# A one-layer hybrid decoder block: the spatial layer norm and some weight halves moved between VectorE and GpSimd, and projections inside the attention tied to its groups

## The chip, the cores and the metric

The kernel runs on one core of a Trainium2 chip. The metric is the device time of one execution in microseconds (us). A core has TensorE (PE, with its weight loads, PEld), VectorE (DVE), ScalarE (ACT), GpSimd (POOL) and SyncE (SP), which here issues nearly all DMAs. Each engine works through its own queue in the order in which the program was built.

## The reference

One decoder layer (DEPTH 1, BATCH 1, SEQ 512, D_MODEL 1024). A normed input goes through one wide projection; three token mixers (sparse attention, spatial gating, RWKV-7) use its columns; their outputs are gated, projected and merged. Cut to what matters here:

```
h = _rmsnorm(x, norm_g)
proj = h @ w_in
nq, nkv, ngate, nz, su, sv, sz, rs, rz, mg = _split_cols(proj)
y_nsa = _nsa(nq, ..., ngate, ...)            # softmax attention, three key sets, gated
# spatial gating of (su, sv):
vn = ((sv - mu) * rsqrt(var + LN_EPS)) * ln_g + ln_b      # over 512 channels
mixed = einsum('gts,bcsgd->bctgd', tril(w_s), vn) + b_s
y_sg = su * mixed
y_rk = _rwkv7(rs, ...)                       # a recurrence over the 512 tokens
ys = stack([y_nsa * silu(nz), y_sg * silu(sz), y_rk * silu(rz)])
zs = einsum('bsnc,ncd->bsnd', ys, w_branch)
x = x + sum(sigmoid(mg) * zs) @ w_o
x = x + sigmoid(_rmsnorm(x) @ w_ple_gate) * (p @ w_ple_proj)
out = _rmsnorm(x)
```

All is float32. With at most 8 blocks of 64 keys and a choice of 16, the selected branch of the attention sees all causal keys.

## The kernel before

**Weights in two halves.** A float32 product is made of three matmuls: each operand is split into a high half (a copy in the type fp32r) and a low half (the rest), and high x high, high x low and low x high are added in PSUM. For weights `wload` does it: SP loads a raw tile `wr` of up to 560 columns (256 KB for 512), ACT casts it to `wh` (L77), and `ph_["l"]`, a variable that holds VectorE (V) or GpSimd (G), subtracts to get `wl` (L78):

```
S.copy(h[:, :m], raw[:, :m])
ph_["l"].tensor_tensor(l[:, :m], raw[:, :m], f(h[:, :m]), OP.subtract)
```

There are four buffers of `wr`, five of `wh` and five of `wl`. `fm_block` makes 128 columns of a projection for all 512 tokens, in 24 matmuls of 512 columns for a depth of 1024 (two weight tiles), 12 for a depth of 512 (one). `tm_chunk` makes up to 280 columns in four row tiles of 128 tokens, 24 matmuls each (four weight tiles). Both write a PSUM tile `mm_ps`, of which there are two, and an evacuation by ACT and VectorE (`evac`) sets it free.

**The stages.** After the norm of x and the setting up of the RWKV part, a loop over eight chunks c of 64 tokens runs the recurrence: r_ps, u_ps and st_ps are its matmuls, L557 and L558 copy u_ps into the state `SV`, L567 to L570 make the new state `tn`, L572 and L573 copy it. Projections (su, sv, six blocks for the merge, sz, rz, nz) stand in the program behind the loop and fill PE between its steps. Their results go to DRAM (`dr`). The spatial gating reads sv back, takes the statistics (L664, L665), adds and takes a power (L667 on VectorE, L668 on GpSimd), normalizes in four row tiles (L670 on VectorE, L671 on GpSimd, L672 on VectorE), mixes (mx_ps), and multiplies by sz. Then y1 and y2, the gated outputs of two branches, are read back and split (L715, L716, L729), while `tm_chunk` makes values and gate (280 columns: L744 to L747 evacuate), and `fm_block` the four query and two key blocks. For sz, and from there on, `ph_["l"]` is GpSimd.

**The attention** loops over query blocks i of 128 tokens in the order 3, 2, 1, 0 (`ATT`), and in each over two groups g of four heads. A group transposes its compressed weights (pc_ps), makes pd, ph and pl of them (L828 to L832), and then, for two key sets b, runs scores (s_ps), maxima on VectorE (L846), exponentials on ACT (L847), scaling (L855, L853), transposes (p_ps), halves (L863, L864) and output matmuls (o_ps). Its last output matmul is kept in the list `anch`, so entries 0 to 7 stand for (3,0), (3,1), (2,0), (2,1), (1,0), (1,1), (0,0), (0,1).

**The merge** runs eight blocks m for each branch, in the order 1, 2, 0. A block is a gate projection of 24 matmuls (for six blocks of branch 1 it was made earlier) and an output projection of 12. Those of branches 1 and 2 need nothing of the attention and can run inside it.

**Order.** The order of each engine's queue is chosen when the program is built: a planner walks through the program with its own cost estimates and gives an engine, of the work that is ready by these, the piece that stands earliest in the program. So what stands later fills gaps. `tc.issue_after(ins)` adds an edge: what the block issues on the engine of `ins` is put behind `ins` in that engine's queue. No engine waits for it. `HOLD` gives such edges to the sixteen blocks of merge 1 and merge 2; -1 means none:

```
hold = [None if h < 0 else anch[h] for h in HOLD]
merge(1, y1H, y1L, True, lambda m: None, hold[:8])
merge(2, y2H, y2L, False, lambda m: None, hold[8:])
```

Of the kernel before, what the change touches and what calls it, by code (L numbers as in the profile page):

```python
# [13 lines left out]
OP = mybir.AluOpType  # L14
# [13 lines left out]
BP = 2  # L28
PS = "VVSG"
ATT = (3, 2, 1, 0)  # L30
HOLD = (-1,) * 12 + (3, 4, 5, 6)
CH = {("nz", 3): 7, ("nz", 2): 5}
LV = (("su", 0), ("su", 1), ("sv", 0), ("sv", 1))
C0 = math.exp(-0.5)
# [5 lines left out]
def f(ap):  # L40
    return ap.bitcast(F32)
# [3 lines left out]
def hybrid_kernel(ctx, tc, x, p, norm_g, w_in, cmp_w1, cmp_w2, cmp_pe, sg_ln_g, sg_ln_b, sg_w, sg_b,  # L45
# [3 lines left out]
    V, S, G, PE, SY = nc.vector, nc.scalar, nc.gpsimd, nc.tensor, nc.sync  # L49
# [10 lines left out]
    def mm(o, a, b, start, stop, **kw):  # L60
        return PE.matmul(o, a, b, start=start, stop=stop, **kw).ins  # L61


    ph_ = {"l": V}
# [16 lines left out]
    def wparts(segs, nk):  # L81
        per = WE // sum(s[2] for s in segs)
        hs, ls = [], []
        for k0 in range(0, nk, per):
            kn = min(per, nk - k0)
            h, l = wload([(w, c0, cn, k0) for w, c0, cn in segs], kn)
            for k in range(kn):
                hs.append(h[:, k, :])
                ls.append(l[:, k, :])
        return hs, ls  # L90
# [58 lines left out]
    def fm_block(c0, n, evac, w=None, srcH=None, srcL=None, nk=8, pool=None):  # L149
        hs, ls = wparts([(w_in if w is None else w, c0, n)], nk)  # L150
        sH, sL = (hH, hL) if srcH is None else (srcH, srcL)
        ps = pmm.tile([128, 512], F32, tag="mm", name="mm_ps")
        for k in range(nk):
            mm(ps[:n], hs[k], sH[:, k, :], k == 0, False)
            mm(ps[:n], hs[k], sL[:, k, :], False, False)
            mm(ps[:n], ls[k], sH[:, k, :], False, k == nk - 1)
        evac(ps)

    def tm_chunk(segs, srcH, srcL, nk, evac):
        n = sum(s[2] for s in segs)  # L160
        hs, ls = wparts(segs, nk)
        for t in range(4):
            ts = slice(t * 128, (t + 1) * 128)
            ps = pmm.tile([128, 512], F32, tag="mm", name="mm_ps")
            for k in range(nk):
                mm(ps[:, :n], srcH[:, k, ts], hs[k], k == 0, False)
                mm(ps[:, :n], srcH[:, k, ts], ls[k], False, False)
                mm(ps[:, :n], srcL[:, k, ts], hs[k], False, k == nk - 1)
            evac(t, ps)
# [368 lines left out]
    for c in range(8):  # L538
# [40 lines left out]
        if u == 1:  # L579
            t = c // 2  # L580
# [25 lines left out]
    for nm, off in (("su", O_SU), ("sv", O_SV)):  # L606
        for hf in range(2):
            ph_["l"] = V if (nm, hf) in LV else G
            def ev_t(t, ps, nm=nm, hf=hf):
                st = stp.tile([128, 512], F32, tag="st", name="st")  # L610
                if nm == "sz":
                    S.activation(st[:, 0:256], ps[:, 0:256], AF.Tanh, scale=0.5)
                    V.scalar_tensor_tensor(st[:, 0:256], st[:, 0:256], 1.0, ps[:, 0:256], op0=OP.add, op1=OP.mult)
                else:
                    S.copy(st[:, 0:256], ps[:, 0:256])
                SY.dma_start(dr[nm][t * 128:(t + 1) * 128, hf * 256:hf * 256 + 256], st[:, 0:256])
            tm_chunk([(w_in, off + 256 * hf, 256)], hH, hL, 8, ev_t)
    for m in range(NG):
# [5 lines left out]
        with ExitStack() as es:  # L624
            if ("sg", m) in CH:
                es.enter_context(tc.issue_after(canch[CH["sg", m]]))
            fm_block(O_MG + 1024 + m * 128, 128, ev_m)

    for nm, off in (("sz", O_SZ),):
        for hf in range(2):  # L630
            def ev_t(t, ps, nm=nm, hf=hf):
                st = stp.tile([128, 512], F32, tag="st", name="st")
                if nm == "sz":
                    S.activation(st[:, 0:256], ps[:, 0:256], AF.Tanh, scale=0.5)
                    V.scalar_tensor_tensor(st[:, 0:256], st[:, 0:256], 1.0, ps[:, 0:256], op0=OP.add, op1=OP.mult)
                else:
                    S.copy(st[:, 0:256], ps[:, 0:256])
                SY.dma_start(dr[nm][t * 128:(t + 1) * 128, hf * 256:hf * 256 + 256], st[:, 0:256])
            tm_chunk([(w_in, off + 256 * hf, 256)], hH, hL, 8, ev_t)
    sg_ctx = ExitStack()  # L640
    sp = sg_ctx.enter_context(tc.tile_pool(name="sp", bufs=2))

    z0 = sp.tile([128, 512], F32, tag="z", name="z0", bufs=1)
    lng = sp.tile([128, 512], F32, tag="lng", name="lng", bufs=1)
# [12 lines left out]
    vn = sp.tile([128, 4, 512], F32, tag="vn", name="vn", bufs=1)  # L657
# [10 lines left out]
    G.tensor_tensor(rs4, rs4, mhalf[:, 0:4], OP.pow)  # L668
    for t in range(4):
        V.tensor_scalar(vn[:, t, :], vn[:, t, :], mv[:, t, 0:1], rs4[:, t:t + 1], op0=OP.subtract, op1=OP.mult)  # L670
        G.tensor_tensor(vn[:, t, :], vn[:, t, :], lng, OP.mult)  # L671
        V.tensor_tensor(vn[:, t, :], vn[:, t, :], lnb, OP.add)  # L672
    for g in range(8):
        ps = rps.tile([128, 4, 64], F32, tag="s", name="mx_ps")
# [64 lines left out]
    vst = nsa.tile([128, 4, 2, 2, 128], R, name="vst")  # L739
    gate = nsa.tile([128, 4, 24], F32, name="gate")  # L740

    def ev_v(t, ps):
        pv = ps[:, 0:256].rearrange("p (b g d) -> p b g d", b=2, g=2)
        S.copy(vst[:, t, :, :, 0:64], pv)  # L744
        V.tensor_tensor(vst[:, t, :, :, 64:128], pv, f(vst[:, t, :, :, 0:64]), OP.subtract)
        S.activation(gate[:, t, :], ps[:, 256:280], AF.Tanh, scale=0.5)  # L746
        V.tensor_scalar(gate[:, t, :], gate[:, t, :], 0.5, 0.5, op0=OP.mult, op1=OP.add)  # L747
    tm_chunk([(w_in, O_NVS, 128), (w_in, O_NVW, 152)], hH, hL, 8, ev_v)

    for q in range(4):  # L750
# [8 lines left out]
    for b in range(2):  # L759
# [7 lines left out]
                V.tensor_tensor(K[o, g, 1, :], ps[a], f(K[a, g, 0, :]), OP.subtract)  # L767
        fm_block((O_NKS, O_NKW)[b], 128, ev_k)


    gp = ctx.enter_context(tc.tile_pool(name="gp", bufs=2))
    macc = gp.tile([128, 8, 512], F32, name="macc", bufs=1)

    def merge(b, yH, yL, first, fin, after=()):
        for m in range(8):
          with ExitStack() as es:
            if m < len(after) and after[m] is not None:
                es.enter_context(tc.issue_after(after[m]))
            sg = gp.tile([128, 512], F32, tag="sg", name="sg")
            if b == 1 and m < NG:  # L780
                SY.dma_start(sg, dr["sg"][m * 128:(m + 1) * 128, :])
            else:
                fm_block(O_MG + b * 1024 + m * 128, 128, lambda ps: S.activation(sg, ps, AF.Tanh, scale=0.5))

            def ev_b(ps):
                if first:
                    V.scalar_tensor_tensor(macc[:, m, :], sg, 1.0, ps, op0=OP.add, op1=OP.mult)
                else:
                    V.scalar_tensor_tensor(sg, sg, 1.0, ps, op0=OP.add, op1=OP.mult)
                    G.tensor_tensor(macc[:, m, :], macc[:, m, :], sg, OP.add)  # L790
                fin(m)
            fm_block(m * 128, 128, ev_b, w_branch[b], yH, yL, 4)
# [84 lines left out]

    hold = [None if h < 0 else anch[h] for h in HOLD]
    merge(1, y1H, y1L, True, lambda m: None, hold[:8])
# [116 lines left out]
```

## Time and profile before

| | |
|---|---|
| runs before, median of 3 | 758.17 us (757.32 to 758.94) |
| the profiled execution's own time | 759.87 us |
| its span, first to last instruction | 758.2 us |
| PE busy | 721.1 us, 95% |
| DVE, ACT, POOL busy | 398.1, 353.1, 326.4 us |
| mean granted TensorE clock | 0.99 of full speed |

Busy time is that in which an engine works on an instruction; issuing and waiting do not count. Matmuls are pipelined and their ends are modelled, so that PE counts as busy as long as they follow closely. What is left of the span on PE is idle time, and the profile names what ended each stretch of it. Durations in the rows are of one execution.

### The profile page before, as it was taken

The numbers are of one execution on the slowest core, as the hardware profiler recorded it, in microseconds if no ns is written. First come the engines' busy times: TensorE is split into PE (matmuls) and PEld (weight loads), VectorE is DVE, ScalarE is ACT, GpSimd is POOL, SyncE is SP. The second block draws the span as 40 slices with busy tenths as digits, with TensorE's granted clock in tenths as the row PEclk, the third lists the DMA queues.
The fourth block names the chain that finished last, engine by engine and source line by source line (L and its number), as shares of the span: only waits on it lengthen the run. The fifth ranks groups of instructions, "written<-read, shape, count | busy, mean of one in ns | idle before, by whom it ended". The sixth has DMA issues, their size and how long they took to land.

```text
span 758.2 us, 13296 instructions
## 1 busy us (share of the span) xinstructions
PE 721.1 (95%) x5053; PEld 611.6 (81%) x5053; DVE 398.1 (53%) x747; ACT 353.1 (47%) x743; POOL 326.4 (43%) x304
## 2 busy tenths in 40 slices
PE   4999999999997999998999999989999999999996
PEld 4878788999876987777777777867877888998995
DVE  6531688658917453456448456487664222216335
ACT  6454565533361332334455555466654333227453
POOL 6445731020335343433545334534345656256563
PEclk9999999999999999999999999999999999999998
DMA  6853222233553354346533222311127433232222
GB/s 199 187 128 94 57 71 67 65 102 113 154 159 125 95 165 116 94 134 182 144 94 111 59 54 57 83 29 42 43 51 239 128 95 112 71 98 74 81 70 112
DMA packets 106690, 78.75 MB, mean 104 GB/s; under 512 B 5569, under 2 KB 97282, under 8 KB 106626
## 3 DMA queue, kind: packets, MB, share of 16 engines
q1 hardware_dynamic: 105890, 75.27, 35.5%
q10 hardware_dynamic: 736, 2.63, 0.8%
q8 instruction: 40, 0.66, 0.4%
q14 instruction: 24, 0.20, 0.1%
HBM read 67.91 MB, written 9.96 MB: 103 GB/s over the span
## 4 chain that ended last, share of the span: by engine, by line
PE 44%; DVE 5%; DMA 2%; ACT 2%; issue 1%; POOL 0%; ACTq 0%; SPq 0%; POOLq 0%; DVEq 0%
PE mm_ps L61 37%; PE s_ps L61 3%; PE o_ps L61 2%; PE p_ps L860 2%; DMA zs<-dr_nz 1%; DVE mx L846 1%; DVE vt L729 1%; DVE pl L864 1%; DVE ysL L716 1%; DVE pl L832 0%; DMA dr_nz<-st 0%; PE sc_c L61 0%; DMA zs<-dr_rz 0%; DMA zs<-dr_y 0%; DVE nsaY L885 0%
## 5 line engine op out<-in xcount | busy, mean ns | idle before, releaser
L78 POOL TENSOR_TENSOR wl<-wr,wh 128x512 fp32r<-128x512 f32 (+1 forms) x168 | 224.0, 1342 | 297.4 <-ACT wh L77 284.0
L77 ACT CAST wh<-wr 128x512 fp32r<-128x512 f32 (+1 forms) x194 | 119.1, 620 | 163.4 <-PE mm_ps L61 112.6
L61 PE MATMUL mm_ps<-hH,wh 128*128 128x512 f32 (+1 forms) x440 | 174.9, 397 | 5.4 <-ACT wh L77 2.1
L61 PE MATMUL mm_ps<-hL,wh 128*128 128x512 f32 (+1 forms) x440 | 172.5, 392 | 0.0
L61 PE MATMUL mm_ps<-hH,wl 128*128 128x512 f32 (+1 forms) x440 | 171.6, 390 | 0.0
L61 PEld LDWEIGHTS mm_ps<-hH,wh 128*128 128x128 f32 x440 | 83.6, 190 | 23.8 <-ACT gate L746 2.6
L61 PEld LDWEIGHTS mm_ps<-hH,wl 128*128 128x128 f32 x440 | 83.5, 190 | 17.4 <-issue 0.2
L61 PEld LDWEIGHTS mm_ps<-hL,wh 128*128 128x128 f32 x440 | 83.7, 190 | 16.6 <-issue 0.2
L61 PE MATMUL mm_ps<-wh,hH 128*128 128x256 f32 (+1 forms) x224 | 64.4, 289 | 1.1 <-ACT gate L746 1.1
L61 PE MATMUL mm_ps<-wh,hL 128*128 128x256 f32 (+1 forms) x224 | 64.8, 290 | 0.0
L61 PE MATMUL mm_ps<-wl,hH 128*128 128x256 f32 (+1 forms) x224 | 64.2, 287 | 0.0
L61 PEld LDWEIGHTS mm_ps<-wh,hH 128*128 128x128 f32 x224 | 42.3, 190 | 2.7 <-ACT gate L746 1.3
L61 PEld LDWEIGHTS mm_ps<-wh,hL 128*128 128x128 f32 x224 | 42.5, 190 | 0.9 <-issue 0.5
L61 PEld LDWEIGHTS mm_ps<-wl,hH 128*128 128x128 f32 x224 | 42.6, 190 | 0.6
L864 DVE TENSOR_TENSOR pl<-p_ps,ph 128x512 fp32r<-128x512 f32 x40 | 27.2, 685 | 25.2 <-ACT ph L863 25.0
L61 PE MATMUL mm_ps<-ysH,wh 128*128 128x512 f32 x96 | 38.6, 402 | 0.8 <-ACT ysH L715 0.8
L61 PE MATMUL mm_ps<-ysL,wh 128*128 128x512 f32 x96 | 38.4, 400 | 0.2 <-DVE ysL L716 0.2
L61 PE MATMUL mm_ps<-ysH,wl 128*128 128x512 f32 x96 | 38.2, 398 | 0.0
L847 ACT ACTIVATE P<-s_ps,mx 128x512 f32<-128x512 f32 (+3 forms) x64 | 33.4, 532 | 7.9 <-DVE mx L846 5.6
L61 PE MATMUL mm_ps<-wh,mH 128*128 128x256 f32 x128 | 36.1, 287 | 0.6 <-DVE x L909 0.6
L61 PE MATMUL mm_ps<-wl,hT 128*128 128x256 f32 x128 | 35.8, 281 | 0.0
L61 PE MATMUL mm_ps<-wl,mH 128*128 128x256 f32 x128 | 35.8, 281 | 0.0
(336 smaller groups left out, 1435.7 us busy)
## 6 DMA issues: line engine op xcount, KB each, us to landing
wr<-in_w_in_dram SPq DMA_DIRECT2D x130, 256.0 KB
wr<-in_w_branch_dram SPq DMA_DIRECT2D x24, 256.0 KB
wr<-in_w_o_dram SPq DMA_DIRECT2D x16, 256.0 KB
wr<-in_w_ple_gate_dram SPq DMA_DIRECT2D x16, 256.0 KB
xs__129<-in_x_dram SPq DMA_DIRECT2D x4, 512.0 KB
w1t<-in_cmp_w_dram SPq DMA_DIRECT2D x4, 512.0 KB
x<-in_x_dram ACTq DMA_DIRECT2D x4, 512.0 KB
out_dram<-x SPq DMA_DIRECT2D x8, 256.0 KB
```

The source lines that it names most:

```text
L61: return PE.matmul(o, a, b, start=start, stop=stop, **kw).ins
L77: S.copy(h[:, :m], raw[:, :m])
L78: ph_["l"].tensor_tensor(l[:, :m], raw[:, :m], f(h[:, :m]), OP.subtract)
L716: V.scalar_tensor_tensor(l, src, sc, f(h), op0=OP.mult, op1=OP.subtract)
L729: V.scalar_tensor_tensor(vt[:, q, :], vt[:, q, :], pc("lnx_b", q), zs, op0=OP.add, op1=OP.mult)
L846: V.tensor_reduce(mx[:, hh:hh + 1], s_ps[:, :W], axis=AX.X, op=OP.max, negate=True)
L847: S.activation(P[:, hh, :W], s_ps[:, :W], AF.Exp, bias=mx[:, hh:hh + 1], accum_out=sm[:, hh:hh + 1])
L860: PE.transpose(p_ps[:, hh * 128:hh * 128 + 128], P[:, hh, kt * 128:kt * 128 + 128], ident)
L864: V.tensor_tensor(pl, p_ps, f(ph), OP.subtract)
```

## The change

The subtraction for the low halves of sz (eight weight tiles) and of values, gate, queries and keys (sixteen) goes from GpSimd to VectorE; between the two places, for rz and nz, and after them it is GpSimd again. The multiplication by the layer norm's gain (L671) goes to VectorE. In `HOLD` the first four blocks of merge 2 get edges: block 0 behind entry 0, block 1 behind entry 1, blocks 2 and 3 behind entry 2. Blocks 4 to 7 keep theirs, and merge 1 has none as before.

```diff
-HOLD = (-1,) * 12 + (3, 4, 5, 6)
+HOLD = (-1,) * 8 + (0, 1, 2, 2, 3, 4, 5, 6)
...
+    ph_["l"] = V
     for nm, off in (("sz", O_SZ),):
...
             tm_chunk([(w_in, off + 256 * hf, 256)], hH, hL, 8, ev_t)
+    ph_["l"] = G
     sg_ctx = ExitStack()
...
         V.tensor_scalar(vn[:, t, :], vn[:, t, :], mv[:, t, 0:1], rs4[:, t:t + 1], op0=OP.subtract, op1=OP.mult)
-        G.tensor_tensor(vn[:, t, :], vn[:, t, :], lng, OP.mult)
+        V.tensor_tensor(vn[:, t, :], vn[:, t, :], lng, OP.mult)
         V.tensor_tensor(vn[:, t, :], vn[:, t, :], lnb, OP.add)
...
     gate = nsa.tile([128, 4, 24], F32, name="gate")
+
+    ph_["l"] = V
 
     def ev_v(t, ps):
...
         fm_block((O_NKS, O_NKW)[b], 128, ev_k)
 
+    ph_["l"] = G
```

## Rows read from the trace of the kernel before

**Rows 1.** The page's first part: engine, busy us (share), instructions.
```profile
span 758.2 us, 13296 instructions
...
PE 721.1 (95%) x5053; PEld 611.6 (81%) x5053; DVE 398.1 (53%) x747; ACT 353.1 (47%) x743; POOL 326.4 (43%) x304
```

**Rows 2.** Waits of PE, whole span: us in total, times, longest.
```profile
PE r_ps L61 <- DVE SV L572: 4.6, 2, 4.3
...
PE mm_ps L61 <- ACT gate L746: 3.0, 3, 1.7
...
PE st_ps L61 <- DVE SV L557: 1.3, 1, 1.3
```

**Rows 3.** Sums by window: length, busy PE, PEld, DVE, ACT, POOL, clock, DMA.
```profile
216.00:242.00 26.00, 20.44 (x223) 16.79 (x219) 12.00 (x21) 7.60 (x15) 13.28 (x10) 0.92 0.58 173
242.00:344.00 102.00, 101.62 (x1045) 86.18 (x1042) 46.45 (x100) 33.71 (x68) 41.55 (x30) 0.99 0.43 121
344.00:366.00 22.00, 18.97 (x141) 16.64 (x140) 14.88 (x24) 10.48 (x24) 7.37 (x5) 1.00 0.54 158
...
468.40:500.30 31.90, 31.59 (x163) 24.96 (x162) 17.64 (x36) 16.53 (x38) 15.71 (x13) 1.00 0.27 71
500.30:512.80 12.50, 10.56 (x69) 7.96 (x68) 11.12 (x29) 8.97 (x26) 3.29 (x3) 1.00 0.04 12
512.80:531.10 18.30, 16.73 (x92) 13.04 (x91) 13.95 (x34) 11.23 (x32) 7.42 (x6) 1.00 0.16 44
...
576.00:758.20 182.20, 172.44 (x1130) 155.28 (x1128) 63.71 (x118) 75.34 (x153) 97.22 (x87) 0.99 0.34 107
```

**Rows 4.** Time line of DVE, 214 to 332: start, us, instruction [idle before].
```profile
229.08 0.69 DVE L664 BATCH_NORM_STATS2 bs<-vn 128x6 f32<-128x512 f32 x1 [11.25 <-DMA vn<-dr_sv]
...
234.58 4.77 DVE L670 TENSOR_SCALAR vn<-vn,mv,rs 128x512 f32<-128x512 f32 x4 [1.19 <-POOL rs L668]
239.27 0.41 DVE L567 TENSOR_TENSOR tn<-st_ps,Dt 128x256 f32<-128x256 f32 x1
```

**Rows 5.** Instructions on tile vn: ns minimum/median/maximum, first and last start.
```profile
L670 DVE TENSOR_SCALAR vn<-vn,mv,rs x4: 540/1482/1510, 234.6 to 237.9; 128x512 f32<-128x512 f32 x4
L671 POOL TENSOR_TENSOR vn<-vn,lng x4: 1437/1469/3116, 236.2 to 240.4; 128x512 f32<-128x512 f32 x4
L672 DVE TENSOR_TENSOR vn<-vn,lnb x4: 673/674/1749, 240.5 to 243.6; 128x512 f32<-128x512 f32 x4
```

**Rows 6.** Line L78, whole span; last the idle time before it (us, times).
```profile
L78 POOL TENSOR_TENSOR wl<-wr,wh x168: 1272/1304/2442, 21.3 to 741.0; 128x512 fp32r<-128x512 f32 x164, 128x560 fp32r<-128x560 f32 x4
...
L78 DVE TENSOR_TENSOR wl<-wr,wh x26: 664/686/1789, 16.7 to 191.7; 128x512 fp32r<-128x512 f32 x26
...
  ACT wh L77: 290.8, 117
```

**Rows 7.** Time line of DVE, 330 to 396.
```profile
354.42 2.46 DVE L729 SCALAR_TENSOR_TENSOR vt<-vt,par,zs 128x512 f32<-128x512 f32 x2 [0.52 <-DMA zs<-dr_rz]
...
357.14 0.73 DVE L729 SCALAR_TENSOR_TENSOR vt<-vt,par,zs 128x512 f32<-128x512 f32 x1
...
358.41 1.80 DVE L729 SCALAR_TENSOR_TENSOR vt<-vt,par,zs 128x512 f32<-128x512 f32 x1
```

**Rows 8.** Line L747: ns minimum/median/maximum.
```profile
L747 DVE TENSOR_SCALAR gate<-gate x4: 166/174/1267, 347.5 to 364.6; 128x24 f32<-128x24 f32 x4
```

**Rows 9.** The chain of waits, from 364 on: start, us, what.
```profile
375.95 5.64 PE mm_ps L61 x24
```

**Rows 10.** Sums of the instructions on tile mm_ps alone, four stretches of the attention.
```profile
440.60:468.40 27.80, 18.43 (x72) 13.17 (x72) 1.36 (x2) 1.19 (x2) 1.00 0.21 56
468.40:500.30 31.90, 21.82 (x86) 15.88 (x86) 2.03 (x3) 1.80 (x3) 1.00 0.27 71
500.30:512.80 12.50, 0.00 (x0) 0.03 (x1) 0.00 (x0) 0.00 (x0) 1.00 0.04 12
512.80:531.10 18.30, 9.53 (x36) 6.47 (x36) 0.69 (x1) 0.59 (x1) 1.00 0.16 44
```

## The prediction

> **What bounds the kernel now.** I read the page's busy shares first, then the waits of PE, then the engines' sums stage by stage, then VectorE's time line in the stages where PE idles. The page shows PE busy for 721.1 of 758.2 us [rows 1]: the matmuls fix most of the time, and a change that adds no matmul can only move the 37 us in which PE idles. PE's waits say what it idles for: 4.6 us for the copy of the recurrent state (L572), 1.3 us for L557 before it, 3.0 us for the evacuation of the gate projection (L746) [rows 2]. The stage sums put idle time in time [rows 3]: 5.56 us in 216 to 242 (20.44 busy of 26.00), only 0.38 in 242 to 344, 3.03 in 344 to 366, and in the attention 0.31, 1.94 and 1.57 us in three successive stretches. Nearly 10 us lie behind 576, where the change touches nothing. So it has to be judged in three places.
>
> **Part one: the spatial layer norm and the low halves of sz.** Near 229 VectorE has stood 11.25 us at the head of its queue for the reload of sv; then come the statistics, and after them four normalizations (L670), 4.77 us. Only then comes L567, which feeds L572, which PE waits for [rows 4]. L567 starts in the moment in which the last L670 ends, so the queue holds it, not its input. Of the L670 the shortest took 0.540 us and the median 1.482 us, while GpSimd's multiplications (L671) take 1.4 to 3.1 us in the same place [rows 5]. The change moves L671 to VectorE. The nearest row there, an addition of two SBUF operands of the same size (L672), has 0.674 us at the median. Without GpSimd beside it a row tile then costs 0.54 + 0.67 + 0.67 = 1.9 us, against 4.77 us for the four L670 alone now.
>
> What matters is how many of the now twelve instructions the planner puts ahead of L567. None: L572 ends before PE comes to the state's matmuls, and the whole wait of 4.3 us goes. All twelve: 4 x 1.9 = 7.6 us in the place of 4.77, 2.8 us more waiting. The planner takes the oldest work that is ready by its own costs; by these four short instructions fitted in front, and the three of the first row tile fill about as much. I take three: L567 comes 4.77 - 1.9 = 2.8 us sooner, rounded down.
>
> Against that stand the eight low halves of sz. On GpSimd one took 1.304 us at the median; on VectorE, where 26 others of that shape are made now, 0.686 [rows 6]. I count two that fall due between 218 and 233. Ahead of the statistics in VectorE's queue they cost nothing, since the 11.25 us wait covers them; without that cover, behind the statistics and ahead of L557, they cost 2 x 0.7 = 1.4 us. I take the middle, 0.7. The first sum: -2.8 + 0.7 = -2.1 us, bounds -4.3 and 2.8 + 1.4 = +4.2. In 242 to 344 the other low halves are put at nothing: PE idles 0.38 us in 102, because sz, rz and nz projections stand between the steps of the recurrence; if that cover went, each would cost its 0.7.
>
> **Part two: the low halves of gate, value, query and key.** Sixteen go to VectorE (four of 128x560, twelve of 128x512). In 344 to 366 PE waits three times for the evacuation by ACT and VectorE (L744 to L746). The first wait hangs on a reload that stays. In front of the other two, VectorE's two-operand instructions are stretched: two L729 take 2.46 us and one 1.80, against one in 0.73 between them [rows 7], and a gate scaling of 24 columns took 1.267 us, where the shortest has 0.166 [rows 8]. I lay the stretching on GpSimd's low halves in this stage, as with L670. At the free prices 2.46 becomes 1.46, and one low half of 0.7 now stands between: 0.3 us of the second wait are saved. Ahead of the third wait 1.80 + 1.27 becomes 0.73 + 0.17, 2.2 us saved, against two or three low halves of 0.7, which saves the third wait, the shortest: the longest, the second, has 1.7 of the 3.0, so 1.3 are left for the first and the third, and I give the third 0.3. Together -0.6 us. Bounds: -2.0, the second and third wait gone wholly, and +1.4, two low halves more ahead of an evacuation and no stretching gone. From 366 to 393 I put nothing: PE works on query and key blocks of 24 matmuls in 5.64 us [rows 9], and two low halves for each block, 1.4 us, hide behind that.
>
> Weighed against a rule: VectorE is busy 14.88 of 22.00 us in 344 to 366 [rows 3]; four low halves more make it 17.6, 80%. The Trainium skill (Perfetto Trace Analysis, Optimizing Scalar/DVE Operations) says that work may be moved off a saturated VectorE to ScalarE or even GpSimd, the reverse of this edit, and that between these two it may not help, since they share a port. By the first half this stage takes its upper bound, the sum -1.4 us; by the second it takes the value above, -3.4. The stretched rows speak for the second.
>
> **Part three: the projections inside the attention.** Eight groups run (query blocks 3 to 0, two head groups each), with projection matmuls between their steps. In the stretches that end with the last output matmul of groups two to five, PE did 72, 86, 0 and 36 of these [rows 10]. Without edges merge 2's blocks 0 to 3 are used up in the third group's stretch, and the fourth runs bare, VectorE busy 11.12 of 12.50 us [rows 3]. The new edges put block 0 behind group one, 1 behind group two, 2 and 3 behind group three; 4 to 7 stay. I count block 0 and 27 matmuls of block 1 or merge 1 in group two's 72, so only blocks 1, 2 and 3 move: about 45, then 36, 72, 36. Each block brings three weight loads, casts and low halves, an addition on GpSimd, and its loads; the edge holds PE alone, so the loads run ahead until the buffers are full, and SP then holds back only further weight loads.
>
> The fourth stretch loses its 1.94 us. The third now has 36 matmuls like the fifth, and begins with a new query block like the fifth; I give it the fifth's idle time, 1.57 us in the place of 0.31. Sum: -1.94 + 1.26 = -0.7 us. Bounds: -2.3, all idle time of both gone, and +2.7: the second and third stretch bare for half of some 20 us, at 1.94 per 12.50, lose 1.55 us each, the second twice that for its longer rows, together 4.65, less 1.94.
>
> **Sum.** -2.1 - 0.6 - 0.7 = -3.4 us. The profiled execution has a span of 758.2 us and a time of 759.87; the median of the runs is 758.17. The sum, made in the span, goes to the median: 754.8 us.
>
> **The rivals.**
> (a) VectorE's queue blocks on a low half. GpSimd idled 290.8 us for ACT's cast in 117 waits, 2.5 us each [rows 6]; there only other low halves stand behind. On VectorE the copies of the recurrence do. The price is that of the one such case now: the reload of sv ahead of L557 costs PE 1.3 + 4.3 = 5.6 us [rows 2, 4]. One more case in sz, with the present one unmended, gives 758.2 + 5.6 - 1.3 = 762.5 us. It decides once a cast comes later than the projections between two steps last, some 3 to 5 us. Against it: the 26 low halves on VectorE so far cost it few long ones (median 0.686).
> (b) All twelve norm instructions go ahead of L567: 2.8 + 0.7 - 1.3 = +2.2, 760.4 us. The planner's costs decide, which no row shows.
> (c) The edges starve groups two and three: 2.7 - 2.7 = 0, 758.2 us. Against it: at 0.235 us a matmul the second has 27.8 - 27 x 0.235 = 21.5 us of PE work left, and the third 31.6 - 50 x 0.235 = 19.8 beside 17.6 of VectorE.
> (d) The change does not do what it says: places come out of the planner's costs anew, gains and losses cancel, 758 us.
> (e) VectorE becomes the bound in 344 to 366, the first half of the rule: 1.4 - 2.8 = -1.4, 756.8 us.
> (f) Every part at its good bound: -4.3 - 2.0 - 2.3 = -8.6, 749.6 us.
>
> **How the numbers follow.** Chances: forecast 0.50, (a) 0.14, (b) 0.10, (c) 0.07, (d) 0.06, (e) 0.04, (f) 0.09. About 0.2%, 1.5 us, is what a measurement tells from no change. Faster: the forecast, (f), (e), and a little of (c) and (d), 0.66. Slower: (a) and six tenths of (b), 0.20. Same: 0.14. The range goes from 749.5, which takes in (f), to 760.5, which takes in (b) and leaves out (a). The forecast's own range is 751.5 to 757.5.
>
> **What would show it.** Right: PE's wait for L572 falls from 4.3 to between 1 and 2 us; no L670 takes over 0.6; the waits at L746 shrink; the projections number about 45, 36, 72, 36, and the fourth stretch has no idle PE. Wrong: VectorE waits for an ACT cast with L557 or L569 behind it; twelve norm instructions in a row ahead of L567; more than 2 us of idle PE in the second or third stretch. The stretch from 576 to the end should keep its 182 us; if it does not, I have overlooked something that moves.

## The result

| | before | after |
|---|---|---|
| median of the runs | 758.44 us, 4 runs (757.32 to 758.94) | 765.70 us, 4 runs (764.05 to 769.00) |
| the profiled execution's span | 758.2 us | 763.4 us |
| mean granted TensorE clock in it | 0.990 | 0.983 |

The ratio is 1.008, 95% interval 1.005 to 1.0109: slower, by 5.2 us between the two profiled spans. 754.8 was forecast, and 765.7 lies outside the range.

### The profile page after: what moved, and what is told of

The parts are those of the page before. It is cut to its first block, busy times and chain, and to the rows that moved or that the text cites. A ratio compares the mean times of both kernels' runs of the same rounds, so it can differ in the third digit from the quotient of the medians.

```text
span 763.4 us, 13289 instructions
## 1 busy us (share of the span) xinstructions
PE 724.4 (95%) x5053; PEld 614.7 (81%) x5053; DVE 405.4 (53%) x775; ACT 353.5 (46%) x743; POOL 286.6 (38%) x276
## 4 chain that ended last, share of the span: by engine, by line
PE 81%; DMA 6%; DVE 6%; ACT 2%; issue 2%; SPq 2%; POOL 0%; ACTq 0%; POOLq 0%; DVEq 0%
PE mm_ps L61 64%; PE s_ps L61 3%; PE o_ps L61 2%; PE g_ps L61 2%; PE p_ps L865 2%; DMA w1t<-in_cmp_w_dram 2%; DMA wr<-in_w_in_dram 1%; PE Yp L61 1%; DMA zs<-dr_nz 1%; DMA vn<-dr_sv 1%; DMA dr_nz<-st 1%; DVE pl L869 1%; PE r_ps L61 1%; PE u_ps L61 1%; DVE pl L837 1%
## 5 line engine op out<-in xcount | busy, mean ns | idle before, releaser
L78 POOL TENSOR_TENSOR wl<-wr,wh 128x512 fp32r<-128x512 f32 x144 | 190.7, 1333 | 302.6 <-ACT wh L77 284.9
L78 DVE TENSOR_TENSOR wl<-wr,wh 128x512 fp32r<-128x512 f32 (+1 forms) x50 | 37.8, 766 | 26.1 <-ACT wh L77 26.1
L851 DVE TENSOR_REDUCE mx<-s_ps 128x1 f32<-128x512 f32 (+3 forms) x64 | 30.1, 482 | 11.3 <-PE s_ps L61 11.1
```

Source lines behind the costliest of these rows:

```text
L851: V.tensor_reduce(mx[:, hh:hh + 1], s_ps[:, :W], axis=AX.X, op=OP.max, negate=True)
```

## The profile after, against the rows of before

The page's first part, against [rows 1]: PE is busy 3.3 us longer on the same 5053 matmuls, so part of the loss is matmuls that ran slower, and the other 1.9 us are idle time. VectorE has 28 instructions more and is busy 7.3 us longer.

```profile
span 763.4 us, 13289 instructions
...
PE 724.4 (95%) x5053; PEld 614.7 (81%) x5053; DVE 405.4 (53%) x775; ACT 353.5 (46%) x743; POOL 286.6 (38%) x276
```

PE's waits (us in total, times, longest), against [rows 2]. The gate's three waits have become one of 2.4 us, and L557 stands as it did. L572 has two waits as before, but they are 1.5 us in the second step of the recurrence and 2.3 in the last, in the place of 4.3 and 0.3. VectorE's halving of the attention's weights (L833, L837) has come up, and the transposes of the mixing's weights (ws_ps) wait 1.0 us for VectorE's L658, which stands behind the norm's additions.

```profile
PE r_ps L61 <- DVE SV L572: 3.8, 2, 2.3
PE o_ps L61 <- DVE pl L837: 3.3, 3, 1.2
...
PE mm_ps L61 <- ACT gate L750: 2.4, 1, 2.4
...
PE p_ps L865 <- DVE pd L833: 1.8, 2, 0.9
PE st_ps L61 <- DVE SV L557: 1.4, 1, 1.4
...
PE ws_ps L657 <- DVE wsT L658: 1.0, 1, 1.0
```

The sums by window, against [rows 3]: length, busy PE, PEld, DVE, ACT, POOL, granted clock, DMA share, GB/s. The four attention windows are the stretches that the prediction calls the second to the fifth.

```profile
216.00:242.00 26.00, 22.96 (x262) 19.43 (x262) 16.29 (x32) 8.27 (x16) 2.63 (x2) 1.00 0.62 196
242.00:344.00 102.00, 98.23 (x994) 82.04 (x996) 45.83 (x107) 33.38 (x66) 27.58 (x20) 0.97 0.39 115
...
331.90:338.70 6.80, 6.28 (x50) 5.12 (x45) 2.62 (x7) 1.09 (x3) 0.32 (x1) 0.50 0.00 0
344.00:366.00 22.00, 19.62 (x143) 18.27 (x142) 14.41 (x30) 9.26 (x22) 0.00 (x0) 0.92 0.53 152
441.90:466.60 24.70, 24.11 (x134) 19.19 (x132) 16.16 (x30) 15.04 (x34) 10.99 (x8) 1.00 0.23 62
466.60:489.30 22.70, 19.70 (x101) 14.23 (x100) 15.76 (x34) 11.80 (x29) 7.78 (x6) 1.00 0.13 35
489.30:514.90 25.60, 25.60 (x138) 21.19 (x138) 12.77 (x29) 14.60 (x36) 10.91 (x10) 1.00 0.17 45
514.90:534.60 19.70, 17.51 (x98) 13.76 (x97) 14.29 (x34) 11.01 (x31) 8.65 (x8) 1.00 0.23 64
580.90:763.40 182.50, 172.51 (x1130) 155.36 (x1128) 63.97 (x118) 75.42 (x153) 97.30 (x87) 0.99 0.33 107
```

Idle PE, window by window. In 216 to 242 it fell from 5.56 to 3.04 us, in 344 to 366 from 3.03 to 2.38. In 242 to 344, where 0.38 us stood, there are 3.77. In the attention's second to fifth stretch it was 0, 0.31, 1.94 and 1.57 us; now it is 0.59, 3.00, 0 and 2.19. The end keeps its 182 us. So idle time changed by -2.52 - 0.65 + 3.39 = +0.22 us ahead of the attention and by +1.96 inside it. Of the 3.39 in 242 to 344, 2.5 belong to the last step of the recurrence and 0.95 to the wait for L658, at 242.0 to 242.9.

The rest is the clock. For 6.8 us from 331.9 on PE had half of it (0.50, the 1.2 GHz level), and two stretches of 3.4 us more (355.8 and 564.1, both 0.51). Before had two of 3.4 us up to 366, at 217.2 and 241.1, both 0.50; the first is scatter between executions, since e1, e4 and e6 below, which change nothing ahead of it, have full clock there. PE's time line from 324 to 345, start, us, instruction, shows what stood before the long one and what it costs:

```profile
330.43 0.30 PE L61 MATMUL r_ps<-SV,Gt 128*64 128x64 f32 x2 [2.32 <-DVE SV L572]
...
333.69 1.57 PE L61 MATMUL Yp<-SV,Gt 128*64 128x64 f32 x16 [0.52 <-DVE SV L557]
...
336.21 0.63 PE L61 MATMUL mm_ps<-hH,wl 128*128 128x512 f32 x1
336.63 0.63 PE L61 MATMUL mm_ps<-hH,wh 128*128 128x512 f32 x1
...
339.00 0.39 PE L61 MATMUL mm_ps<-hH,wh 128*128 128x512 f32 x1
339.24 0.39 PE L61 MATMUL mm_ps<-hL,wh 128*128 128x512 f32 x1
```

PE stood 2.32 us for the state's copy (L572) in the last step of the recurrence, then 0.52 for L557, and matmuls of 512 columns started 0.43 us apart in the place of 0.23 until 338.7. At that rate 3.4 us at half clock lose 3.4 x (1 - 0.23 / 0.43) = 1.6 us. Up to the attention after has 3.4 us more of it than before: 0.22 + 1.6 = 1.8 us, and the first matmul of the attention (sc_c) starts 1.4 us later, at 371.37. Inside the attention 1.96 us of idle time and the stretch at 564.1, another 1.6, make 3.6 us; the attention takes 209.53 us from sc_c to its last output matmul, against 205.95. With 0.2 us behind it that is the 5.2.

The spatial layer norm is where it was meant to be, but the step of the recurrence beside it gets no shorter. VectorE's time line:

```profile
234.09 1.92 DVE L672 TENSOR_SCALAR vn<-vn,mv,rs 128x512 f32<-128x512 f32 x4 [0.91 <-POOL rs L670]
235.92 0.68 DVE L673 TENSOR_TENSOR vn<-vn,lng 128x512 f32<-128x512 f32 x1
236.52 0.42 DVE L567 TENSOR_TENSOR tn<-st_ps,Dt 128x256 f32<-128x256 f32 x1
236.85 1.28 DVE L673 TENSOR_TENSOR vn<-vn,lng 128x512 f32<-128x512 f32 x2
...
239.59 0.28 DVE L572 COPY SV<-tn 64x256 f32<-64x256 f32 x1
```

Four normalizations take 1.92 us where [rows 4] has 4.77, one multiplication stands with them, and L567 starts at 236.52, 2.75 us sooner than in [rows 4]. PE, however, waits for L572. Between L567 and L572 VectorE now has four more instructions of the norm, three multiplications and an addition, where before it had none: L572 starts at 239.59, before at 239.93. Below, the kernel before (L572, PE's last matmul ahead of the state's matmuls, and these), then PE in the kernel after:

```profile
239.93 0.68 DVE L572 COPY SV<-tn 64x256 f32<-64x256 f32 x1
236.19 0.28 PE L61 MATMUL mm_ps<-wh,hL 128*128 128x256 f32 x1
240.76 0.90 PE L61 MATMUL r_ps<-SV,Gt 128*64 128x64 f32 x16 [4.28 <-DVE SV L572]
...
238.21 0.28 PE L61 MATMUL mm_ps<-wl,hH 128*128 128x256 f32 x1
240.01 0.69 PE L61 MATMUL r_ps<-SV,Gt 128*64 128x64 f32 x16 [1.52 <-DVE SV L572]
```

From the copy of u_ps (L557, at 230.63 before and at 229.50 after) to r_ps the step takes 10.1 us before and 10.5 after. PE's wait in it fell by 2.76 us all the same: 0.75 because r_ps comes sooner, and 2.0 because PE has 44 projection matmuls of 256 columns to run ahead of it, where it had 21. PE runs the same 5053 matmuls in both, so what runs here is missing later.

The projection matmuls in the third, fourth and fifth stretch, against [rows 10]; the second has 50:

```profile
466.60:489.30 22.70, 9.26 (x36) 6.64 (x36) 0.69 (x1) 0.59 (x1) 1.00 0.13 35
489.30:514.90 25.60, 17.58 (x72) 13.31 (x72) 1.38 (x2) 1.19 (x2) 1.00 0.17 45
514.90:534.60 19.70, 9.06 (x36) 6.56 (x36) 0.69 (x1) 0.59 (x1) 1.00 0.23 64
```

The third stretch shows what becomes of 36. VectorE's time line, 468 to 492:

```profile
476.89 0.69 DVE L794 SCALAR_TENSOR_TENSOR sg<-sg,mm_ps 128x512 f32<-128x512 f32 x1 [3.70 <-PE pc_ps L829]
477.50 0.68 DVE L833 TENSOR_TENSOR pd<-pc_ps,hm 128x512 f32<-128x512 f32 x1
478.87 1.53 DVE L837 TENSOR_TENSOR pl<-pd,ph 128x512 fp32r<-128x512 f32 x1 [0.69 <-ACT ph L836]
...
482.82 0.69 DVE L869 TENSOR_TENSOR pl<-p_ps,ph 128x512 fp32r<-128x512 f32 x1 [1.22 <-ACT ph L868]
```

The last eighteen of the 36 run in one piece from 472.36 to 476.6, ahead of the transposes (pc_ps) of the group's compressed weights, while VectorE stands 3.70 us. Then pd, ACT's ph and pl follow one another (L833, L836, L837) and no projection is left to run beside them: PE waits 0.91 us for pd and 1.06 for pl. Before, the stretch had 86 projections; VectorE stood longer there, 3.34 and 4.16 us for ph, and PE idled 0.31 us in all [rows 3].

## The experiments

The kernels were timed in three sets, each with the kernel before beside it on one chip (the first four, the next four and the last four of the table); before had medians of 759.58, 759.43 and 759.56 us there. In the table, idle is idle PE in 216 to 366 by the window sums; sc_c the start of the attention's first matmul; attention the time from there to its last output matmul. The first iv_ps, ahead of all that is changed, starts at 205.89 to 206.94 in these traces, so starts scatter by 1 us.

```
                                    us      ratio  95% interval     idle  sc_c    attention
before                                                              8.97  369.97  205.95
after                               765.70  1.0080 1.0050 - 1.0109  9.19  371.37  209.53
e1  edges alone                     763.41  1.0048 1.0031 - 1.0065  9.84  369.05  208.95
e2  VectorE edits alone             761.54  1.0028 1.0008 - 1.0048  9.99  371.25  205.79
e3  L671 alone                      760.97  1.0017 1.0000 - 1.0035 11.17  372.69  205.78
e8  e2, nz block 3 a step earlier   763.32  1.0054 1.0038 - 1.0071 14.00  373.56  205.84
e4  gate to keys alone              758.87  0.9985 0.9970 - 1.0001  8.36  369.07  207.65
e5  sz alone                        761.45  1.0022 1.0005 - 1.0039 11.91  370.70  205.85
e6  other edges alone               757.60  0.9975 0.9963 - 0.9987  9.74  368.39  203.31
e9  e2, nz block 2 a step later     754.63  0.9930 0.9914 - 0.9946  7.56  365.88  205.78
e10 e9 with e6's edges              753.85  0.9919 0.9897 - 0.9941  4.77  365.86  203.22
e11 nz block 2 a step later alone   762.07  1.0025 1.0012 - 1.0037  9.76  371.02  207.50
e12 e10, sz left on GpSimd          759.25  0.9989 0.9976 - 1.0002  9.65  370.94  203.25
e13 e10, nz block 1 held too        751.35  0.9887 0.9867 - 0.9907  6.40  363.30  203.22
```

### The change in two halves (e1, e2)

e1 is the kernel before with the new edges, e2 is after with the old ones:

```diff
 e1, in the kernel before:
-HOLD = (-1,) * 12 + (3, 4, 5, 6)
+HOLD = (-1,) * 8 + (0, 1, 2, 2, 3, 4, 5, 6)
 e2, in the kernel after:
-HOLD = (-1,) * 8 + (0, 1, 2, 2, 3, 4, 5, 6)
+HOLD = (-1,) * 12 + (3, 4, 5, 6)
```

> The kernel before with the new HOLD alone. Theory A (the edges starve the third group): the stretch that ends with group (2,0) gets 36 projection matmuls in the place of 86 and idles about 3.0 us of PE, in the place of 0.31; the fourth loses its 1.94; with the smaller waits the kernel takes 761 to 763 us. Rival C (the loss in the attention of the changed kernel follows from what comes before it, the edges by themselves are harmless or good): 757 to 759 us.

> The kernel before with the three VectorE edits (layer norm multiplication, low halves of sz, low halves of gate, value, query and key) and the old HOLD. Theory A (two separate losses): the attention's third and fourth stretch are as before, the first score matmul of the attention comes about 1.4 us later than before, 759 to 760.5 us. Rival C (all of the loss is in these edits): 762 to 766 us. A third possibility, the forecast of these parts: 755 to 756.5 us.

Both halves cost, 0.48% and 0.28%, and make after's 0.8% together. In the table they act in different places: e1 leaves the start of sc_c within that scatter and lengthens the attention by 3.0 us; e2 starts sc_c 1.3 us later and leaves the attention alone. e1's windows for the third and fourth stretch, and for a stretch at half clock inside the third, behind PE's waits for pd (0.91 us) and pl (1.06):

```profile
464.30:488.00 23.70, 21.06 (x102) 15.42 (x101) 15.87 (x34) 11.85 (x29) 7.88 (x6) 0.93 0.14 34
488.00:513.60 25.60, 25.60 (x139) 21.19 (x138) 12.72 (x29) 14.59 (x36) 10.91 (x10) 1.00 0.18 46
...
478.60:482.00 3.40, 3.24 (x12) 2.62 (x12) 1.32 (x3) 1.21 (x4) 0.00 (x0) 0.50 0.01 2
```

The third idles 2.64 us on 36 projections, and here half clock follows at 478.6; in after the same two waits are followed by full clock. The fourth, on 72, idles 0. e2's windows have after's picture ahead of the attention, nearly line by line:

```profile
216.00:242.00 26.00, 21.99 (x214) 18.47 (x207) 16.67 (x33) 7.57 (x16) 2.35 (x2) 1.00 0.66 198
242.00:344.00 102.00, 98.59 (x1004) 82.39 (x1006) 45.74 (x106) 33.05 (x66) 27.58 (x20) 0.97 0.41 114
344.00:366.00 22.00, 19.43 (x137) 18.04 (x133) 13.99 (x30) 9.32 (x22) 0.00 (x0) 0.92 0.53 155
```

### The VectorE edits one by one (e3, e5, e4)

Each is the kernel before with one line or one pair of lines of the change:

```diff
 e3:
-        G.tensor_tensor(vn[:, t, :], vn[:, t, :], lng, OP.mult)
+        V.tensor_tensor(vn[:, t, :], vn[:, t, :], lng, OP.mult)
 e5 (ahead of sz, and of the gating), e4 (ahead of the values, and behind the keys):
+    ph_["l"] = V
...
+    ph_["l"] = G
```

> The kernel before with the layer norm multiplication on VectorE alone. Theory A (an earlier layer norm lets the mixing run earlier, and its matmuls are then missing as filling work in the last step of the recurrence): the wait for L572 near 236 falls from 4.3 us to about 2, the last step idles some 2 to 3 us, 757.5 to 760 us in all. Rival B (the low halves of sz in VectorE's queue do the harm): no idle PE at the last step, 755 to 756.5 us.

> The kernel before with the low halves of sz on VectorE alone. Theory A: some of the filling work of the last step is used earlier here too (3.8 us planned there in the place of 6.3), a small loss, 758.5 to 761 us. Rival B (VectorE's queue waits for a cast with the recurrence's copies behind it): PE waits for L557 or L569 over 1 us somewhere in 242 to 325, 761 to 764 us.

> The kernel before with the low halves of gate, value, query and key on VectorE alone. The prediction's part two, alone: the waits for L746 fall by about 0.6 us, 758 to 759.5 us. Rival E (VectorE becomes the bound of 344 to 366): waits longer by 1.4 us, 760.5 to 762 us.

e4 costs nothing, and in its own stage, 344 to 366, idle time falls from 3.03 to 1.49 us. e3 and e5 cost about 0.2% each. In e3 idle time falls by 2.4 us in 216 to 242 (to 3.15) and rises by 4.0 in 242 to 344 (to 4.36), but 1.3 us of that rise are the rest of one wait, for L572, from 240.31 to 243.27. That wait is shorter than before (2.96 us against 4.28) although the step has become longer, 12.4 us from L557 to r_ps: the four L670 still take 3.84 us beside GpSimd's low halves of sz, and ten of the twelve norm instructions stand ahead of L572. The last step then idles 1.6 us. e5 has its loss in the first window (7.78 in the place of 5.56), where PE waits 2.71 us for L557 and 5.08 for L572, and 1.6 us just ahead of the last r_ps, for L684. In e5 the four normalizations take 3.82 us beside GpSimd's multiplications; only with both edits are they down to 1.92. A wait over 0.3 us for L557 or L569, which the rival wanted between 242 and 325, does not show. The three add up to e2 within their intervals: 0.17 + 0.22 - 0.15 = 0.24%.

### What fills the last step of the recurrence (e9, e8)

The norm ends 3 us sooner in after (242.3 in the place of 245.3), but the mixing (mx_ps) runs from 251.9 to 301.4 in the place of 280.9 to 323.5 (starts of the first and the last matmul): the planner, by its own costs, sets it into the third to fifth step. Below, the starts of r_ps in steps 4 to 7 (counted from 0, so 7 is the last), and the projection matmuls between u_ps of step 6 and r_ps of step 7:

```
            r_ps 4   r_ps 5   r_ps 6   r_ps 7   projections ahead of r_ps 7
before      279.72   298.70   316.29   331.24   24 (321.6 to 331.2)
after       281.37   301.75   319.32   330.43    3 (324.7 to 330.4)
e9          282.23   302.62   317.88   329.55   24 (319.8 to 329.5)
```

After's steps 4 to 6 have more work between them than the recurrence's chain needs, and the last has nearly none. In the kernel before, two nz blocks are held back by edges behind steps 5 and 7 (`CH`). e9 and e8 are e2 with one of them moved by one step:

```diff
 e9:
-CH = {("nz", 3): 7, ("nz", 2): 5}
+CH = {("nz", 3): 7, ("nz", 2): 6}
 e8:
-CH = {("nz", 3): 7, ("nz", 2): 5}
+CH = {("nz", 3): 6, ("nz", 2): 5}
```

> The three VectorE edits with the old HOLD, and the third nz block held one step of the recurrence longer (behind step 6 and not behind step 5), so that about 5 us of projection leave the steps before and stand in the last one; nothing is taken from behind the recurrence. Theory A2 (filling work is used up too early inside the recurrence, since steps that need some 8 us are filled with 17, and is missing in its last step): the last step's idle PE, 2.8 us, falls below 1.2, no new wait of PE at 343 to 353, 756 to 759.5 us. Rival B2 (idle time of PE only wanders, the sum is fixed by the chain of the recurrence and of what follows it): 760.5 to 763 us, with the idle time at another place between 300 and 366.

> The three VectorE edits with the old HOLD, and the last nz block let go one step of the recurrence earlier (behind step 6 and not behind step 7), so that 5.6 us of projection can fill the last step. Theory A: PE's idle time between 325 and 344, about 2.8 us, is gone or below 0.7, and the clock there stays near full; 754.5 to 757 us, 2.5 to 4 us under the same kernel without this. Rival B (the recurrence is late because of VectorE's queue, not for want of filling work): within 1 us of the same kernel without it.

e9 is 0.7% faster than before, some 1% faster than e2, by one number. Its windows:

```profile
242.00:344.00 102.00, 99.78 (x1052) 83.59 (x1049) 48.07 (x113) 33.60 (x67) 27.59 (x20) 1.00 0.43 121
344.00:366.00 22.00, 20.65 (x119) 17.73 (x118) 15.44 (x29) 11.16 (x25) 0.00 (x0) 1.00 0.63 191
```

The 2.32 us in the last step are gone, and the clock is granted in full from 216 to 366. Against before that is 1.4 us less idle time and 6.8 us less at half clock, 3.2 us by the rate above (half of it the scatter at 217.2); sc_c starts 4.1 us sooner. What e9 doesn't mend are the 0.95 us for L658 and the second step, which takes 10.5 us from L557 to r_ps as in after. e8 went against its expectation. It fills the last step just as well, but with the block that had stood behind it, and what follows the recurrence runs bare:

```profile
325.00:344.00 19.00, 18.43 (x183) 15.51 (x179) 7.24 (x18) 5.13 (x10) 0.00 (x0) 1.00 0.31 92
343.00:353.00 10.00, 2.40 (x34) 1.98 (x34) 5.37 (x14) 3.03 (x6) 1.64 (x1) 0.74 0.33 106
347.80:358.00 10.20, 5.30 (x46) 5.11 (x47) 7.22 (x17) 4.48 (x10) 0.00 (x0) 0.50 0.33 107
```

PE waits 5.1 us for yc (L596) and then 4.2 for the gate's evacuation (L750), which stands on ACT behind the splits of y1 (L717), with 10.2 us at half clock over it. So the loss goes where the fill is missing. Most of it is no price of the VectorE instructions themselves, which are the same in e2, e8 and e9, but of the order around them.

### Which edges (e6)

e6 is the kernel before with block 2's edge moved from entry 2 to entry 1, against e1:

```diff
-HOLD = (-1,) * 12 + (3, 4, 5, 6)
+HOLD = (-1,) * 8 + (0, 1, 1, 2, 3, 4, 5, 6)
```

> The kernel before with edges for merge 2's blocks 0 to 3 behind groups one, two, two and three (the change has one, two, three, three): 72 projection matmuls for the third group, 36 for the fourth. Theory A (the loss is the uncovered chain pc_ps, pd, ph, pl at the head of query block 2 when only 36 are left for it): the third group idles below 0.7 us and the fourth below 0.7, 757 to 759.5 us, 3 us or more under the kernel with the change's HOLD alone. Rival D (any edge that makes the second group run with less filling work costs, or edges as such): 761 to 763.5 us.

Its windows for the third to the fifth stretch, in which 72, 36 and 36 projections run:

```profile
463.70:491.30 27.60, 27.55 (x141) 21.41 (x140) 17.16 (x36) 15.44 (x35) 12.90 (x10) 1.00 0.23 58
491.30:510.00 18.70, 18.04 (x108) 14.89 (x107) 12.70 (x30) 11.54 (x30) 7.38 (x6) 1.00 0.17 44
510.00:527.00 17.00, 16.06 (x90) 12.72 (x89) 12.56 (x32) 10.69 (x29) 7.33 (x6) 1.00 0.18 47
```

With 72 projections the third idles 0.05 us, and with 36 the fourth 0.66 and the fifth 0.94. One digit between e1 and e6 is worth 0.7%. The fourth stretch can live on 36, and the third can't. That the third begins a new query block doesn't explain it alone: the fifth begins one too and idles 0.94 us here on 36.

### Together, and crossed (e10 to e13)

e10 is after with e9's `CH` and e6's `HOLD`; e11 is the kernel before with e9's `CH` alone; e12 is e10 without the lines of sz; e13 is e10 with a third nz block held:

```diff
 e13:
-CH = {("nz", 3): 7, ("nz", 2): 6}
+CH = {("nz", 3): 7, ("nz", 2): 6, ("nz", 1): 5}
```

> All three VectorE edits, the second held nz projection moved one step later (5 to 6), and the edges 0, 1, 1, 2 in the place of 0, 1, 2, 2. If the two gains add (the held nz projection with the VectorE edits gave -0.7%, the edges 0, 1, 1, 2 alone -0.25%): ratio to before 0.9905, about 752 to 753 us, no idle PE over 2 us between 242 and 344, the fourth attention stretch without idle PE over 0.7. If the attention group edges lose their effect because the attention starts 4 us earlier and its loads come no sooner: 0.993 to 0.995, 754.5 to 756 us.

> The kernel before with only the held nz projection moved from step 5 to step 6. Theory 'the gain repairs what the VectorE edits took from the last step of the recurrence': before has some 6 us of other matmuls in its last step already, so little to gain: ratio 0.998 to 1.001, 757.5 to 759.5 us. Rival 'the move is worth its own gain in any kernel, by shortening the overfilled fifth and sixth steps': 0.993 to 0.996, 754 to 756.5 us.

> As the kernel with all repairs, but the low halves of sz stay on GpSimd. If sz's edit costs by itself (+0.2% when made alone): 0.2% under the kernel with all repairs, 751 us, ratio 0.988 to 0.989. If its cost was the bare last step of the recurrence, which the held projection now fills: the same as that kernel within 0.15%; or slower, if sz's edit is what brings the mixing forward.

> As the kernel with all repairs, with the first nz projection held behind step 5 as well. If overfilled steps four to six still delay the end of the recurrence: up to 1 us faster than that kernel, ratio 0.989. If the last steps are now all covered: within 0.15% of it. If work then runs short in the third and fourth step: slower, by the idle PE that shows there.

e10 is at 0.9919, between the sum of the two gains (0.9905) and the 0.993 to 0.995 of the other expectation, and its interval reaches both. By the table the gains add: sc_c starts as early as in e9, and the attention is as short as in e6. The fourth stretch idles 0.65 us.

e11 went as neither theory had it: 0.25% slower. The move pays with the VectorE edits and not alone. Alone it takes the block out of a step that had use for it: idle PE in 242 to 344 rises from 0.38 to 1.34 us. Of its loss 1.0 us stands ahead of the attention (1.9 counted from the first iv_ps, which came 0.8 us sooner than in before); the other 1.5 are in the attention, most of it in its last two groups, where nothing was changed. Half clock shows there in e11 (0.53 in 561.6 to 565.0), as in e4 (0.50 from 560.3) and after (0.51 from 564.1), and not in before (1.00 from 546 to 576).

e12 shows that sz's edit, which costs 0.2% alone, is worth 0.7% in company. Without it the last step is filled, but 344 to 353 runs bare:

```profile
344.00:353.00 9.00, 5.19 (x55) 4.73 (x54) 5.21 (x13) 3.47 (x9) 0.00 (x0) 0.77 0.63 194
```

PE waits 3.8 us there for the gate's evacuation and the clock is 0.77. The last of the three expectations held: without sz's edit the mixing starts at 271.3 in the place of 253.0, and the order that e10's edges suit is another one again. Alone the edit doesn't bring it forward (282.8 in e5, 280.9 before); with L671 it does.

e13 is the fastest kernel here, 751.35 us, 0.9887 of before, faster than both kernels of the case. Its sc_c comes 2.6 us before e10's, more than the 1 us expected, but that is not the held block alone: the first iv_ps came 0.5 us sooner, and e10's trace has half clock for 3.4 us from 217.2 and again near 241, where e13's has full clock. From r_ps 5 to r_ps 7 e13 takes 26.2 us and e10 27.0. The intervals of the two ratios overlap a little, so e13's lead over e10 is the least certain of these results.

## Why the prediction was wrong, by its own steps

**Part one, near 229: the sum came out, the step did not.** "L567 comes 4.77 - 1.9 = 2.8 us sooner": 2.75. "I take three" of the twelve ahead of it: there were five, four normalizations (L672 after the change) and one multiplication, 2.43 us in the place of 1.9, and they began 0.5 sooner. None of the four took over 0.55 us without GpSimd beside it. The low halves of sz cost about what was put: two of them stand among the statistics, and from the first statistic to the first normalization it takes 6.14 us in the place of 5.50. But PE waits for L572, and the prediction counted what stands ahead of L567 alone. Nine of the twelve stand ahead of L572, which starts 0.34 us sooner, and the step became 0.4 us longer. That -2.1 was forecast and idle time fell by 2.5 us is luck: of the 2.76 us by which the wait for L572 fell, 2.0 are projections run earlier, and they are missing later.

**Part one, 242 to 344: the step that failed first.** "In 242 to 344 the other low halves are put at nothing: PE idles 0.38 us in 102, because sz, rz and nz projections stand between the steps of the recurrence; if that cover went, each would cost its 0.7." The cover was taken as a property of the stage. It is a supply: the same matmuls, dealt out over seven steps. The edits moved the mixing 29 us forward and projections into earlier steps; the last step had 3 projections in the place of 24, and PE idled 2.5 us more in it and ran at half clock after it. Another 0.95 us is the wait for L658. e9, whose one number gives the 24 back, turns +0.28% into -0.70%, with the mixing where after has it (from 252.8). Not the low halves' 0.7 us but the bare chain of the recurrence was the price.

**Part two: right in sum, by two errors that cancel.** -0.6 was forecast, and idle PE in 344 to 366 fell by 0.65, with 3.4 us at half clock in it. The second and the third wait, 1.67 and 0.30 us, are gone wholly, which was the bound of -2.0. The first, of which the prediction says that it "hangs on a reload that stays", grew from 1.06 to 2.38: ACT has the evacuation L750 behind L717, and L717's reload landed at 352.3 in the place of 350.3. Alone (e4) the part saves 1.54 us. L729 (L731 after) takes 1.51 us for two and 0.75 for one, against 2.46 and 1.80 in [rows 7]: the stretching is gone, as argued. The Trainium skill (Perfetto Trace Analysis, Optimizing Scalar/DVE Operations) says that work may be moved off a saturated VectorE, and that moving it between VectorE and GpSimd might not help, since they share a port. By the first half, as the prediction weighed it, this stage would have become 1.4 us slower; e4, which moves work onto VectorE there, is at 0.9985, and VectorE is busy 14.74 of 22 us. The second half agrees with the normalization, 1.482 us at the median beside GpSimd's work and 0.542 without.

**Part three: failed by a size.** The term that was mis-sized is the third stretch's. "The fourth stretch loses its 1.94 us": it did. "I give it the fifth's idle time, 1.57 us in the place of 0.31": the third took 3.00, and the second and the fifth, put at nothing, 0.6 more each. Sum +1.96 in the place of -0.7, inside its bound of +2.7; with the clock at 564.1 it was 3.6. What was overlooked: a count doesn't say where the matmuls stand. With 36 projections the fifth idled 1.57 us before, 2.19 in after and 0.94 in e6; in the third of after all 36 are spent 12.7 us before its end, ahead of the chain pd, ph, pl. Rival (c) named the mechanism, with +2.7 us for this part, and the attention became 3.6 us longer.

**The rivals.** (a) did not cost anything that shows: VectorE did stand 7.27 us for a cast ahead of 217.2, with the copies of XT (L527) behind it, but PE has no wait for them between 217 and the first u_ps, at 222.79. (b) came about for the larger part, nine of twelve ahead of L572, and its price was hidden by the projections that ran there. (c) was half of the result. (d) was right that the places come out of the planner's costs anew, and wrong that gains and losses cancel. (e) did not come. None of them had the last step of the recurrence running bare, or a clock that falls. Most signs of being right came (1.5 us for L572, no normalization over 0.6, 50, 36, 72 and 36 projections, no idle PE in the fourth stretch), and of the signs of being wrong the 3.00 us in the third stretch did; no sign watched PE's idle time in 242 to 344.

**What stays open.** Why the planner brings the mixing forward by 9 us for L671 alone (e3), by none for sz alone (e5), and by 29 for all: its costs stand in no trace. Nor does a trace tell how the 23 projections came to stand in the second step, or what the mixing's move alone did to the last. And after's median lies 7.3 us over before's, its profiled span 5.2: the four runs' spans went with the granted clock, 761.9 us at 0.991 and 766.9 at 0.977, and which stalls brought it down in the slowest is open. So is why half clock shows near 562 in some traces and not in others, though PE idles there alike (1.53 us in 546 to 576 before).

## What to carry to other kernels

Where PE is kept busy by work that fills a chain's gaps, a 0.4% idle stage is not slack: count the filling matmuls step by step before and after, because an edit that shifts when work is ready can deal them out anew; here the last step starved. Follow a gain to the instruction that PE waits for (L572), not to one ahead of it (L567), and ask of a wait that shrank whether the chain got shorter or other work was moved into it. After such an edit retune the edges that hold filler back; here one digit in each of two lists turned 0.8% slower into 0.8% faster. Price a starved step by its own chain, with the slower clock behind it, not by the idle time of a stretch that looks alike.

## What the runs showed of the hardware

The granted clock is lost within a kernel that keeps PE 95% busy. In after it was 0.50 for 6.8 us behind 2.32 us of idle PE, in e1 0.50 for 3.4 us in the middle of a stretch with 2.64 us idle, in e8 0.50 for 10.2 us where 7.6 of 10 us were idle (343 to 353); in e9, without a wait over 0.6 us in the recurrence's last step, it stayed at 1.00 there. The idle time alone does not decide: the waits for pd and pl in the third stretch (0.91 and 1.06 us) were followed by 0.50 in e1 and by 1.00 in after, and in e9 a wait of 2.49 us for L557, up to 230.8, left the clock at 1.00. What does decide is open here. At half clock a matmul of 512 columns starts every 0.43 us in the place of 0.23. The Trainium skill (TensorE: Matmul & The Clock Gate, Part 1) has half clock as the state of an idle PE and full clock as that of a busy one. The trace agrees in direction, as 0.50 follows 2.32 us of idle PE in after and is 1.00 again 6.8 us later, with PE at work. In after the half clock behind the 2.32 us cost up to 3.2 us, an estimate by the rate above for 6.8 us, which is more than the stall; a forecast that counts idle time alone misses it.

VectorE's normalization of a 128x512 tile is stretched beside GpSimd: it took 1.482 us at the median in before, and 0.542 in after, where GpSimd has no work at that place. Either kind of GpSimd's work is enough: the four take 3.84 us in e3, beside low halves, and 3.82 in e5, beside multiplications, against 1.92 in after.
